# A transformer layer with 32 experts: small loads moved behind the first projection's input, the last output tiles taken half by half up to the gather, and the overflow path's loads on another queue

## The chip, the cores and the metric

The kernel runs on one core of a Trainium2 chip. The core has five engines with a queue of instructions each: TensorE (PE, with its weight loads as PEld), VectorE (DVE), ScalarE (ACT), GpSimd (POOL) and SyncE (SP). Loads from memory are issued from an engine's queue; here SP issues the large ones and ACT the small ones. The metric is the device time of one execution in microseconds (us).

## The reference

One decoder layer over 256 tokens of width 1024:

```python
mod = silu(c) @ w_ada + b_ada            # shifts, scales and gates
h = x * (1 + scale) + shift              # adaLN
proj = h @ w_in                          # attention, indexer and retention heads
mix = concat(sparse_attention(proj), retention(proj))
x = layer_norm(x * ALPHA + gate * (mix @ w_out))
# top-4 of 32 experts, clamped SwiGLU, 1024 -> 2 x 1024 -> 1024
x = layer_norm(x * ALPHA + gate2 * moe(x))
```

The sparse attention keeps the 64 best keys of a token by an indexer's score and adds a bias by distance. Each expert has 12 MB of weights in float32 (`w_gate_up` 8 MB, `w_down` 4 MB), and all 32 are read once.

## The kernel before

**Front.** TensorE forms the shifts and scales `sha` and `sc1` from eight tiles of `w_ada` of 1 MB (`mod_step`, L163). ACT and DVE then make `h` from `xT` in two parts: `hh` (ACT, L238) is `h` rounded, `hl` (DVE, L240) what rounding lost, over the full value `hfull` (L239). Weights are split the same way into `whi` and `wlo` (`split`, L258 and L259), and `proj_t` adds `whi`·`hh`, `whi`·`hl` and `wlo`·`hh`. The first two tiles so used are `w_idx` (result in `ps_g`, then `wiT`, L313) and the first `w_in` tile (result in `pq`, then `qiT`, L319). The profile gives matmuls the line of their helper `mm`, L110.

**Loads.** `load` issues on SP's queue, `small` on ACT's. Small tensors are loaded at the start: `head`, `hot`, `row`; then `fd` (written to memory, L193) and `bias` (read back from it in another layout, L196), the constants `cst` (L211), `b_ada` (L215) and `rows_` (L217). SP and ACT take eight completion semaphores (DMAHW0 to DMAHW7 in the listings) in turn; a load takes one only when the load that had it before has landed.

**Output and routing.** Four tiles of `w_out` cover pairs of `k`: `out_all(i)` does pair `i` for both halves of the tokens (`s`) and of the width (`j`), with three products for each `k` into `pz[s][j]`. For the last pair a loop over `s` and `j` does `out_proj((6, 7), s, j)`, then `z` (L600, L601), its statistics (L607), its transposes `pn` (L604), `zT`, and the router's logits; for each `s` it then makes the choice of the experts (`msk`, L624), the rank of a token at its expert (`prk` on TensorE, `rk`, L630) and the normalized rows `nh` and `nl` (L633). `dispatch(0)` compares ranks with slots (`oh`, L736) and gathers the first four experts' tokens by matmul (`pg`), copied out as `xe` (L749, L751).

**Experts.** A ring of 17 slots of 1 MB holds weight tiles; `load_up` (L706) and `load_down` (L714) issue a tile when a slot is free. TensorE does `pgate`, `pup` and `py`. After expert 24 a flag `over` is read, and `tc.If` (L960) runs `overflow()` if some expert got more tokens than it has slots for. Ahead of the `If`, the loads of expert 25 and of `w_down` of 24 are issued as `ahead`.

Of the kernel before, what the change touches and what calls it, by code (L numbers as in the profile page):

```python
# [14 lines left out]
OP = mybir.AluOpType  # L15
# [78 lines left out]
def layer(ctx, tc, t, out):  # L94
# [116 lines left out]
    small(out=cst, in_=t["cst"])  # L211
# [91 lines left out]
    with tc.issue_after(first["mod"].ins):  # L303
# [3 lines left out]
    w = w_in("p (k c) -> p k c", k=8)  # L307
    idx = scr6[:, 0:1024].rearrange("p (i c) -> p i c", i=4)
# [263 lines left out]
    out_all(2)  # L572
# [20 lines left out]
    for s in range(2):  # L593
        st = sb("lst", 128, 2, 6, bufs=2)
        pr = ps("s")
        z = acc[:, s]
        for j in range(2):
            js = slice(j * 512, (j + 1) * 512)
            out_proj((6, 7), s, j)
            V.tensor_mul(z[:, js], pz[s][j], ga[:, js])  # L600
            V.scalar_tensor_tensor(z[:, js], xn[s][:, js], ALPHA, z[:, js], op0=OP.mult, op1=OP.add)  # L601
            pn = ps("t", (128, 4, 128), name="pn")
            for b in range(4):
                T.transpose(pn[:, b], z[:, j * 512 + b * 128:j * 512 + (b + 1) * 128], ident)  # L604
            zT = sb("zT", 128, 4, 128, bufs=2)
            A.activation(zT, pn, AF.Copy)
            V.bn_stats(st[:, j], z[:, js])  # L607
            for b in range(4):
                k = 4 * j + b
                mm(pr[:, 0:E], zT[:, b], w_ha[:, k], k == 0, k == 7)  # L610
        mv = sb("lmv", 128, 2, bufs=2)
        V.bn_aggr(mv, st)
        sd = sb("lsd", 128, 2, bufs=2)
# [16 lines left out]
        V.scalar_tensor_tensor(rk[:, s], prk[:, 0:E], 1.0, msk[:, s], op0=OP.add, op1=OP.mult)  # L630
        nl.append(sb(f"nl{s}", 128, D, pool=keep, dt=F32R, tag=f"x{s}"))
        with tc.issue_after(placed.ins):
            V.scalar_tensor_tensor(nl[s], z, sd[:, 0:1], nh[:, s].bitcast(F32), op0=OP.mult, op1=OP.subtract)  # L633
            V.tensor_copy(rstd[:, s:s + 1], sd[:, 0:1])
# [95 lines left out]

    def dispatch(quad):

        e = 4 * quad
        oh = mk.tile([128, 2, 4, CAP], F32R, name="oh", bufs=1)
        for s in range(2):
            V.tensor_tensor(oh[:, s], slots[:, None, :].to_broadcast([128, 4, CAP]),  # L736
                            rk[:, s, e:e + 4, None].to_broadcast([128, 4, CAP]), op=OP.is_equal)
        xes = [mk.tile([128, 8, 128], F32, name="xe", bufs=3) for _ in range(2)]
        pgs = []

        def gather(i, s, start, stop):
# [4 lines left out]
        def take(h, i, engine):
            src = pgs[i // 2][:, i % 2, 128 * h:128 * h + 128]
            if engine is V:
                return V.tensor_scalar(xes[h][:, i], src, ha[:, i:i + 1], hb[:, i:i + 1], op0=OP.mult, op1=OP.add)  # L749
            else:  # L750
                return A.activation(xes[h][:, i], src, AF.Identity, bias=hb[:, i:i + 1], scale=ha[:, i:i + 1])  # L751

        if quad == 0:

            for s in range(2):
                for i in range(8):
                    if s == 0 and i % 2 == 0:
                        pgs.append(ps("t" if i < 4 else "g", (128, 2, 256), name="pg"))
                    gather(i, s, s == 0 and i % 2 == 0, s == 1 and i % 2 == 1)
            for h in range(2):  # L760
                for i in range(8):
                    first[i % 2] = take(h, i, (V, A)[i % 2])
        else:
            for i in range(8):
                if i % 2 == 0:
                    pgs.append(ps("t", (128, 2, 256), name="pg"))
                for s in range(2):
                    gather(i, s, s == 0, s == 1)
            for i in range(8):
                for h in range(2):  # L770
                    take(h, i, (V, A)[h])
# [325 lines left out]
```

## Time and profile before

| what | value |
|---|---|
| runs | 1153.84, 1156.03, 1156.25 us (median 1156.03) |
| the profiled execution | 1154.32 us, span 1152.6 us |
| PE busy | 1048.8 us (91%) |
| DVE, ACT, POOL busy | 358.6, 177.5, 50.9 us |
| moved | 451.99 MB, 392 GB/s on average |

The span runs from the first to the last instruction. The share of busy time is an average over stages with different limits; each stage has to be read by itself, by which wait ends last in it.

### The profile page before, as it was taken

Reading aid. Unit: us, or ns where it says so; the run is one execution under the profiler, and the core shown is the slowest. Engines: PE = TensorE matmul, PEld = TensorE weight load, DVE = VectorE, ACT = ScalarE, POOL = GpSimd, SP = SyncE. Lnnn points to the kernel's source line nnn. Section 1 sums busy time; section 2 is a strip of 40 time slices with the busy share of each in tenths; the row PEclk is TensorE's granted clock in tenths of the full one; section 3 lists DMA queues with packets and bytes.
Section 4 is the critical chain, followed back from the end, with each engine's and each line's share of the span. In section 5 each row is a group of like instructions: output and inputs, shape, how many; then the busy total and the mean of one; then the engine's idle time right before and its main releaser. Section 6 shows DMA issues by size and latency. Waiting matters only on the chain. (4 is left out here: it accounts for less than half of the span.)

```text
span 1152.6 us, 12061 instructions
## 1 busy us (share of the span) xinstructions
PE 1048.8 (91%) x4939; PEld 449.1 (39%) x4939; DVE 358.6 (31%) x665; ACT 177.5 (15%) x292; POOL 50.9 (4%) x38
## 2 busy tenths in 40 slices
PE   7799997999999999999999899989988698999895
PEld 1587686443434333432333233323422133443232
DVE  0586785312222222321222122212221211312125
ACT  1424641400201000100010001000100000200001
POOL 0114210110000000000000000000000000000001
PEclk9799997999999999999999999999999989999998
DMA  9968995799999999999999999999999989999994
GB/s 357 374 238 345 338 397 220 298 412 421 421 421 421 422 421 421 421 422 421 421 422 421 421 422 421 421 422 421 421 421 422 421 331 423 421 421 421 421 418 162
DMA packets 65861, 451.99 MB, mean 392 GB/s; under 512 B 7380, under 2 KB 8573, under 8 KB 11817
## 3 DMA queue, kind: packets, MB, share of 16 engines
q1 hardware_dynamic: 63536, 447.52, 94.3%
q10 hardware_dynamic: 2266, 3.65, 1.0%
q8 instruction: 41, 0.67, 0.2%
q14 instruction: 18, 0.15, 0.0%
HBM read 450.05 MB, written 1.09 MB: 391 GB/s over the span
## 5 line engine op out<-in xcount | busy, mean ns | idle before, releaser
L110 PE MATMUL pgate<-w,xe 128*64 128x512 f32 x1024 | 345.3, 604 | 27.7 <-DMA w<-in_w_gate_up 27.7
L110 PE MATMUL pup<-w,xe 128*64 128x512 f32 x1024 | 352.2, 596 | 0.0
L110 PE MATMUL py<-w,aT 128*64 128x512 f32 (+1 forms) x1056 | 244.0, 592 | 11.1 <-DMA w<-in_w_down 9.4
L110 PEld LDWEIGHTS pgate<-w,xe 128*64 128x64 f32 x1024 | 93.6, 137 | 177.0 <-DMA w<-in_w_gate_up 83.2
L110 PEld LDWEIGHTS pup<-w,xe 128*64 128x64 f32 x1024 | 104.7, 137 | 145.9 <-issue 139.4
L800 DVE TENSOR_SCALAR sw_g<-pgate 128x512 f32<-128x512 f32 x32 | 22.1, 692 | 384.8 <-PE pgate L110 384.8
L110 PEld LDWEIGHTS py<-w,aT 128*64 128x64 f32 x1056 | 71.6, 137 | 140.0 <-issue 93.0
L846 DVE TENSOR_TENSOR y<-py,gf 64x512 f32<-64x512 f32 x62 | 42.7, 688 | 206.5 <-PE py L110 206.1
L801 ACT ACTIVATE act<-sw_g 128x512 f32<-128x512 f32 x32 | 20.2, 630 | 511.4 <-DVE sw_g L800 511.4
L873 DVE TENSOR_TENSOR acc<-acc,psc 128x512 f32<-128x512 f32 x60 | 38.6, 684 | 24.5 <-PE psc L110 24.5
L749 DVE TENSOR_SCALAR xe<-pg,ha,hb 128x128 f32<-128x128 f32 x64 | 25.6, 409 | 57.2 <-PE pg L110 43.8
L1026 POOL TENSOR_TENSOR acc<-acc,ln 128x512 f32<-128x512 f32 (+1 forms) x2 | 2.7, 1340 | 908.1 <-ACT acc L1025 908.1
L110 PE MATMUL pm<-w,cT 128*32 128x512 f32 x192 | 35.8, 726 | 5.8 <-DMA w<-in_w_ada 5.8
L751 ACT ACTIVATE xe<-pg,hb,ha 128x128 f32<-128x128 f32 x64 | 28.4, 458 | 63.8 <-DVE xe L749 63.8
L258 ACT ACTIVATE whi<-w 128x2048 fp32r<-128x2048 f32 (+1 forms) x17 | 31.3, 1839 | 40.2 <-DMA w<-lay_w_in 11.4
L110 PE MATMUL pg<-oh,nh 128*128 128x256 f32 x128 | 35.6, 310 | 1.1 <-DVE oh L736 1.1
L860 ACT ACTIVATE yh<-y,gs 128x1024 fp32r<-128x1024 f32 x15 | 17.2, 1148 | 110.9 <-DVE y L846 110.9
L110 PE MATMUL pg<-oh,nl 128*128 128x256 f32 x128 | 34.2, 298 | 0.0
L829 ACT ACTIVATE aT<-pact 128x512 f32<-128x512 f32 x32 | 19.1, 597 | 98.0 <-PE pact L828 98.0
L110 PE MATMUL psc<-yh,ohT 128*128 128x512 f32 x60 | 24.9, 455 | 10.1 <-ACT yh L860 6.8
L259 DVE TENSOR_TENSOR wlo<-w,whi 128x2048 fp32r<-128x2048 f32 (+1 forms) x14 | 30.9, 2209 | 4.4 <-ACT whi L258 4.2
L110 PEld LDWEIGHTS <-pick 96*64 96x64 bf16 x190 | 15.0, 109 | 44.1 <-issue 40.5
(260 smaller groups left out, 911.0 us busy)
## 6 DMA issues: line engine op xcount, KB each, us to landing
w<-in_w_gate_up SPq DMA_DIRECT2D x256, 1024.0 KB, 19.8
w<-in_w_down SPq DMA_DIRECT2D x124, 1024.0 KB, 19.8
w<-in_w_ada SPq DMA_DIRECT2D x24, 1024.0 KB, 7.0
w<-lay_w_in SPq DMA_DIRECT2D x12, 1024.0 KB, 9.2
w<-lay_w_out SPq DMA_DIRECT2D x4, 1024.0 KB
w<-in_w_down SPq DMA_DIRECT2D x7, 512.0 KB, 17.0
bias<-fd ACTq DMA_DIRECT2D x1, 1024.0 KB, 14.2
xT<-lay_xT SPq DMA_DIRECT2D x1, 1024.0 KB, 8.7
```

What stands on the lines that cost most here:

```text
L110: T.matmul(o, l, r, start=start, stop=stop)
L258: A.activation(hi, w, AF.Copy)
L259: (G if i % 4 == 3 and i < 13 else V).tensor_tensor(lo, w, hi.bitcast(F32), op=OP.subtract)
L749: return V.tensor_scalar(xes[h][:, i], src, ha[:, i:i + 1], hb[:, i:i + 1], op0=OP.mult, op1=OP.add)
L751: return A.activation(xes[h][:, i], src, AF.Identity, bias=hb[:, i:i + 1], scale=ha[:, i:i + 1])
L800: V.tensor_scalar(g, pg, 7.0, None, op0=OP.min)
L801: A.activation(s, g, AF.Sigmoid, scale=1.702)
L829: A.activation(aT, pa, AF.Copy)
L846: V.tensor_mul(y[o:o + CAP, c], py[64 * c:64 * c + 64], gf[64 * c:64 * c + 64, c * 512:(c + 1) * 512])
L860: A.activation(yh, y, AF.Copy, scale=gs)
L873: V.tensor_add(o, o, p_)
L1026: G.tensor_mul(o, o, g2[:, cs])
```

## The change

Five parts. `load_later()` issues `cst`, `fd`, `b_ada`, `rows_` and `bias` behind the copy of `whi` of the first `w_in` tile on ACT. `hh` is made first, half on ACT and half on DVE, and then `hfull` and `hl` in pairs; `proj_t` does all eight products with `hh` before those with `hl`. `out_all(2)` is gone: with TensorE's order written out by hand, `out_proj` takes pairs 2 and 3 (`k` = 4 to 7) for one (`s`, `j`) at a time, and transposes, logits, ranks and both parts of the first gather follow in that order. The overflow path's loads go on POOL's queue. `ahead` is gone.

```diff
+    def load_later():
+        fap = fd[:]
+        small(out=cst, in_=t["cst"])
+        small(out=fd, in_=f8)
+        small(out=b_ada[0:128:32], in_=t["b_ada"])
+        small(out=bias, in_=bass.AP(tensor=fap.tensor, offset=fap.offset, ap=[[1, 128], [384, H], [1, 256]]))
+        small(out=rows_[0:72], in_=t["rows"])
...
     for b in range(8):
         if b % 2 == 0:
-            f2 = sb("hfull", 128, 2, 256, bufs=2, tag="zT")
-        f = f2[:, b % 2]
-        A.activation(hh[:, b], xT[:, b], AF.Identity, bias=sha[:, b:b + 1], scale=sc1[:, b:b + 1])
-        V.tensor_scalar(f, xT[:, b], sc1[:, b:b + 1], sha[:, b:b + 1], op0=OP.mult, op1=OP.add)
-        V.tensor_sub(hl[:, b], f, hh[:, b].bitcast(F32))
+            A.activation(hh[:, b], xT[:, b], AF.Identity, bias=sha[:, b:b + 1], scale=sc1[:, b:b + 1])
+        else:
+            first["h"] = V.tensor_scalar(hh[:, b], xT[:, b], sc1[:, b:b + 1], sha[:, b:b + 1], op0=OP.mult, op1=OP.add)
+    for b in range(0, 8, 2):
+        f2 = sb("hfull", 128, 2, 256, bufs=2, tag="zT")
+        V.tensor_scalar(f2[:, 0], xT[:, b], sc1[:, b:b + 1], sha[:, b:b + 1], op0=OP.mult, op1=OP.add)
+        A.activation(f2[:, 1], xT[:, b + 1], AF.Identity, bias=sha[:, b + 1:b + 2], scale=sc1[:, b + 1:b + 2])
+        V.tensor_sub(hl[:, b:b + 2], f2, hh[:, b:b + 2].bitcast(F32))
...
     w = w_in("p (k c) -> p k c", k=8)
+    with tc.issue_after(first["split"].ins):
+        load_later()
...
     split_wo(3)
-    out_all(2)
...
+    with tc.manual_schedule(engines={mybir.EngineType.PE}):
+        for j in range(2):
+            out_proj((4, 5, 6, 7), 0, j)
+            z_out(0, j)
+        zT0 = z_T(0, 0)
+        out_proj((4, 5), 1, 0)
+        logits(0, 0, zT0)
+        zT1 = z_T(0, 1)
+        out_proj((6, 7), 1, 0)
+        z_out(1, 0)
+        logits(0, 1, zT1)
+        stats(0)
+        out_proj((4, 5), 1, 1)
+        zT0 = z_T(1, 0)
+        out_proj((6, 7), 1, 1)
+        first["z"] = z_out(1, 1)
+        choose(0)
+        logits(1, 0, zT0)
+        rank(0)
+        zT1 = z_T(1, 1)
+        stats(1)
...
+        logits(1, 1, zT1)
+        choose(1)
...
-                        nc.sync.dma_start(out=w, in_=t["w_gate_up"][0, bass.ds(e, 1), k * 128:(k + 1) * 128,
+                        G.dma_start(out=w, in_=t["w_gate_up"][0, bass.ds(e, 1), k * 128:(k + 1) * 128,
...
-        if e == E - 7:
-            wu, wd = ahead
-        else:
-            wu = load_up(e)
-            wd = load_down(e - 1) if e else None
+        wu = load_up(e)
+        wd = load_down(e - 1) if e else None
...
         if e == E - 8:
-            ahead = load_up(e + 1), load_down(e)
             r = nc.values_load(over[0:1, 0:1], min_val=0, max_val=1)
```

On ACT near the start, the rows of before, from the store of `fd` to the load of `rows_` (`pd` is a small matmul's result, DMA a load's issue, the numbers behind names are of buffers):

```order
L193 DMA fd_97<-scr7_69 8x384 [waits DVE_49]
L211 DMA cst_117<-lay_cst 128x1072
L203 ACTIVATE scr8_70<-pd_101 128x256 [waits PE_49]
L196 DMA bias_99<-fd_97 128x8x256 [waits DMAHW5_49]
L203 ACTIVATE scr8_70<-pd_104 128x256 [waits PE_49]
L203 ACTIVATE scr8_70<-pd_107 128x256 [waits PE_49]
L215 DMA b_ada_92<-lay_b_ada 4x1024 [waits DMAHW2_49,Pool_49]
L203 ACTIVATE scr8_70<-pd_110 128x256 [waits PE_49]
L209 ACTIVATE scr9_71<-ps_t_114 128x512 [waits DMAHW3_49,PE_49]
L217 DMA rows__120<-lay_rows 72x512 [waits DMAHW4_49]
```

The five loads stand between the first copies out of TensorE, ahead of the copy of `modrow` that leads to `sha`. In the changed kernel, from the last copies of `hfull`:

```order
L263 ACTIVATE whi_239<-w_237 128x2048 [waits DMAHW5_49]
L244 ACTIVATE hfull_198<-xT_117,sha_176,sc1_177 128x256 [waits DVE_49]
L244 ACTIVATE hfull_202<-xT_117,sha_176,sc1_177 128x256 [waits DVE_49]
L197 DMA cst_115<-lay_cst 128x1072 [waits DMAHW0_49]
L198 DMA fd_97<-scr7_69 8x384
L199 DMA b_ada_92<-lay_b_ada 4x1024 [waits Pool_49]
L201 DMA rows__116<-lay_rows 72x512 [waits DMAHW6_49]
L200 DMA bias_98<-fd_97 128x8x256 [waits DMAHW7_49,DMAHW2_49]
L321 ACTIVATE scr6_72<-ps_g_212 4x256 [waits DVE_49,PE_49]
L327 ACTIVATE scr6_72<-pq_251 128x256 [waits PE_49]
L327 ACTIVATE scr6_72<-pq_251 128x256
L263 ACTIVATE whi_389<-w_387 128x2048
```

They now stand behind `hh`, `hfull` and `whi`, ahead of the copies for `wiT` (L321) and `qiT` (L327), with a wait for `fd` ahead of the load of `bias`; the copy of the next `whi` stands behind the copies of `qiT`.

On TensorE at the end of the output projection, the rows of before from the first transposes of `s`=1 to the gather (`ps_s` the logits, `pn` the transposes, `prk` the rank); the last product `pz` and the rank of `s`=0 stand right ahead of them:

```order
L604 MATMUL pn_1528<-head_73,acc_1288 128x128 [waits PE_49]
L604 MATMUL pn_1528<-head_73,acc_1288 128x128 x3
L604 MATMUL pn_1548<-head_73,acc_1288 128x128 [waits DVE_49]
L604 MATMUL pn_1548<-head_73,acc_1288 128x128
L110 MATMUL ps_s_1519<-w_ha_1330,zT_1533 128x32 [waits Activation_49]
L110 MATMUL ps_s_1519<-w_ha_1330,zT_1533 128x32 x3
L604 MATMUL pn_1548<-head_73,acc_1288 128x128 x2
L110 MATMUL prk_1574<-msk_1453,ones_82 128x32 [waits PE_49]
L110 MATMUL ps_s_1519<-w_ha_1330,zT_1553 128x32 [waits Activation_49]
L110 MATMUL ps_s_1519<-w_ha_1330,zT_1553 128x32 x3
L110 MATMUL prk_1574<-msk_1453,cst_117 128x32 [waits DVE_49]
L110 MATMUL pg_1596<-oh_1591,nh_1289 128x256 [waits DVE_49,PE_49]
```

All of `s`=1's transposes, logits and rank stand behind the last product, and the gather behind both ranks.

Changed, from the last four products to the start of the gather (`pr` now names the logits):

```order
L110 MATMUL pz_1331<-wlo_1407,ch_1176 128x512
L110 MATMUL pz_1331<-whi_1406,ch_1176 128x512
L110 MATMUL pz_1331<-whi_1406,cl_1209 128x512
L110 MATMUL pz_1331<-wlo_1407,ch_1176 128x512
L110 MATMUL pr_1429<-w_ha_1326,zT_1522 128x32 [waits Activation_49]
L110 MATMUL pr_1429<-w_ha_1326,zT_1522 128x32 x3
L110 MATMUL prk_1543<-msk_1425,cst_115 128x32 [waits DVE_49,PE_49]
L615 MATMUL pn_1546<-head_73,acc_1284 128x128 [waits DVE_49,PE_49]
L615 MATMUL pn_1546<-head_73,acc_1284 128x128 x3
L110 MATMUL pr_1429<-w_ha_1326,zT_1551 128x32 [waits Activation_49]
L110 MATMUL pr_1429<-w_ha_1326,zT_1551 128x32 x3
L110 MATMUL pg_1573<-oh_1434,nh_1285 128x256 [waits DVE_49]
```

The transposes of `s`=1's first half stand six products ahead of the logits, the rank of `s`=0 stands right behind the first four logits of `s`=1, and the gather of `s`=0 (`nh`, `nl0`) ahead of the rank of `s`=1.

On SP at the `If`, before, from the last load ahead of it to the false path's jump:

```order
L714 DMA w_4862<-in_w_down 128x2048 [waits DMAHW1_49,PE_49]
L714 DMA w_4864<-in_w_down 128x2048 [waits DMAHW2_49,PE_49]
L959 TENSOR_LOAD over_1585 [waits DVE_49]
L960 COMPARE_AND_BRANCH
...
L960 UNCONDITIONAL_BRANCH [waits DMAHW0_49,DMAHW1_49,DMAHW2_49,DMAHW3_49,DMAHW4_49,DMAHW5_49,DMAHW6_49,DMAHW7_49]
```

The jump past the overflow path waits for all eight completion semaphores, behind twelve loads. Changed:

```order
L783 DMA w_4739<-in_w_down 128x2048 [waits DMAHW6_49,PE_49]
L1009 TENSOR_LOAD over_1623 [waits DVE_49]
L1009 ISA x2
L775 DMA w_5204<-in_w_gate_up 128x2048 [waits DMAHW7_49,PE_49]
L775 DMA w_5206<-in_w_gate_up 128x2048 [waits DMAHW0_49,PE_49]
L775 DMA w_5208<-in_w_gate_up 128x2048 [waits DMAHW1_49,PE_49]
L775 DMA w_5210<-in_w_gate_up 128x2048 [waits DMAHW2_49,PE_49]
L1010 COMPARE_AND_BRANCH
...
L1010 UNCONDITIONAL_BRANCH
L775 DMA w_5212<-in_w_gate_up 128x2048 [waits DMAHW3_49,PE_49]
```

Four loads of the next expert stand between the read of the flag and the branch, the jump waits for nothing, and the other loads stand behind it.

## Rows read from the trace of the kernel before

**Rows 1.** The page, part 4: chain that ended last, by line

```profile
DMA w<-in_w_gate_up 10%; DMA w<-in_w_down 3%; PE py L110 1%; PE pgate L110 1%; PE pup L110 1%; PE p L110 0%; PE pg L110 0%; DVE acc L1021 0%; PE psc L110 0%; DVE acc L1020 0%; DVE y L996 0%; DVE yl L998 0%; ACT yh L997 0%; PE pact L828 0%; DVE fst L1016 0%; SPq L706 0%
```

**Rows 2.** Windows: length, busy us (and count) per engine, TensorE clock, DMA share, GB/s

```profile
0.00:20.00 20.00, 12.89 (x34) 3.72 (x38) 1.26 (x5) 3.02 (x6) 2.86 (x13) 1.00 0.91 365
20.00:30.00 10.00, 7.39 (x38) 1.43 (x38) 0.00 (x0) 0.60 (x1) 0.00 (x0) 1.00 0.88 313
60.00:180.00 120.00, 119.54 (x760) 89.90 (x758) 88.03 (x175) 49.80 (x77) 29.52 (x16) 1.00 0.86 330
200.00:210.00 10.00, 10.00 (x55) 6.24 (x55) 4.42 (x20) 6.43 (x13) 0.00 (x0) 0.84 0.19 66
930.00:940.00 10.00, 10.00 (x48) 3.51 (x47) 0.00 (x0) 0.00 (x0) 0.00 (x0) 0.99 0.69 287
940.00:950.00 10.00, 10.00 (x51) 3.49 (x49) 2.67 (x4) 1.23 (x2) 0.00 (x0) 1.00 0.74 305
960.00:1110.00 150.00, 141.32 (x608) 53.06 (x608) 35.80 (x57) 16.75 (x28) 0.00 (x0) 0.98 1.01 421
```

**Rows 3.** Timeline of SP's DMA queue: start, length, line, count

```profile
17.89 10.82 SPq L163 DMA_DIRECT2D w<-in_w_ada  x2
```

**Rows 4.** Waits of SP, 0 to 40 us: total, times, longest us

```profile
SPq L163 <- DMA bias<-fd: 10.1, 1, 10.1
SPq L163 <- DMA fd<-scr: 5.9, 1, 5.9
```

**Rows 5.** Timeline of ACT and its DMA queue, 0 to 60 us

```profile
9.17 0.29 ACTq L193 DMA_DIRECT2D fd<-scr  x1
...
14.20 0.44 ACTq L196 DMA_DIRECT2D bias<-fd  x1
...
50.70 1.91 ACT L258 ACTIVATE whi<-w 128x2048 fp32r<-128x2048 f32 x1 [3.93 <-PE pq L110]
```

**Rows 6.** Timeline of PE, 26 to 60 us; in brackets the idle time before, and releaser

```profile
25.81 1.58 PE L110 MATMUL pm<-w,cT 128*32 128x512 f32 x11
...
33.23 1.93 PE L110 MATMUL pm<-w,cT 128*32 128x512 f32 x8 [5.84 <-DMA w<-in_w_ada]
...
53.07 1.73 PE L110 MATMUL psc<-scr 64*128 64x128 f32 x16 [1.29 <-ACT scr L319]
```

**Rows 7.** Timeline of DVE, 30 to 60 us

```profile
37.01 0.16 DVE L230 TENSOR_TENSOR sha<-pmt,head 128x8 f32<-128x8 f32 x1
...
42.31 0.75 DVE L240 TENSOR_TENSOR hl<-hfull,hh 128x256 fp32r<-128x256 f32 x2
```

**Rows 8.** Timeline of PE, 170 to 212 us

```profile
185.14 0.40 PE L110 MATMUL pz<-wlo,ch 128*128 128x512 f32 x1
...
188.39 0.38 PE L110 MATMUL prk<-msk,cst 128*128 128x32 f32 x2 [2.85 <-DVE msk L624]
...
198.18 0.55 PE L110 MATMUL pg<-oh,nh 128*128 128x256 f32 x1 [1.13 <-DVE oh L736]
...
204.84 1.03 PE L110 MATMUL pgate<-w,xe 128*64 128x512 f32 x4
```

**Rows 9.** Timeline of DVE, 170 to 212 us

```profile
172.47 2.29 DVE L259 TENSOR_TENSOR wlo<-w,whi 128x2048 fp32r<-128x2048 f32 x1 [0.82 <-ACT whi L258]
...
196.26 1.28 DVE L633 SCALAR_TENSOR_TENSOR nl<-acc,lsd,nh 128x1024 fp32r<-128x1024 f32 x1
...
197.62 0.75 DVE L736 TENSOR_TENSOR oh<-slots,rk 128x256 fp32r<-128x256 f32 x2
```

**Rows 10.** Waits of SP, 900 to 945 us

```profile
SPq L960 <- SPq L960: 19.5, 3, 14.5
```

**Rows 11.** Timeline of SP's DMA queue, 890 to 960 us

```profile
912.54 7.78 SPq L714 DMA_DIRECT2D w<-in_w_down  x4
...
941.22 4.04 SPq L706 DMA_DIRECT2D w<-in_w_gate_up  x8
```

**Rows 12.** Timeline of PE, 900 to 960 us

```profile
924.65 0.64 PE L110 MATMUL pgate<-bias_gu,pick 96*64 96x512 bf16 x2 [5.27 <-PEq L960]
```

More of the change, by code (lines that the diff above doesn't have):

```diff
@@ L302, in layer @@
     load(out=w, in_=t["w_idx"])
-    with tc.issue_after(first["mod"].ins):
+    with tc.issue_after(first["mod"].ins), tc.issue_after(first["h"].ins):
         w = [d.rearrange("p (k c) -> p k c", k=8) for d in split(w)]
@@ L592, in layer @@
     rstd = sb("rstd", 128, 2, pool=keep)
[L593 to L613, printed above, removed]
+    prs = [ps("s", name="pr") for _ in range(2)]
@@ L630, in layer, with low, one_hot, gather @@
         V.scalar_tensor_tensor(rk[:, s], prk[:, 0:E], 1.0, msk[:, s], op0=OP.add, op1=OP.mult)
+    def low(s):
         nl.append(sb(f"nl{s}", 128, D, pool=keep, dt=F32R, tag=f"x{s}"))
-        with tc.issue_after(placed.ins):
-            V.scalar_tensor_tensor(nl[s], z, sd[:, 0:1], nh[:, s].bitcast(F32), op0=OP.mult, op1=OP.subtract)
-            V.tensor_copy(rstd[:, s:s + 1], sd[:, 0:1])
+        V.scalar_tensor_tensor(nl[s], acc[:, s], sds[s][:, 0:1], nh[:, s].bitcast(F32), op0=OP.mult, op1=OP.subtract)
+    def one_hot(quad, s):
+        V.tensor_tensor(oh[:, s], slots[:, None, :].to_broadcast([128, 4, CAP]),
+                        rk[:, s, 4 * quad:4 * quad + 4, None].to_broadcast([128, 4, CAP]), op=OP.is_equal)
+    def gather(i, s, start, stop):
+        for n in (nh[:, s], nl[s]):
+            mm(pgs[i // 2][:, i % 2], n[:, i * 128:(i + 1) * 128], oh[:, s].rearrange("p e c -> p (e c)"),
+               start and n is not nl[s], stop and n is nl[s])
+    oh = sb("oh", 128, 2, 4, CAP, pool=keep, dt=F32R)
+    with tc.manual_schedule(engines={mybir.EngineType.PE}):
[19 more added lines that the diff above has]
+        stats(1)
+        with tc.issue_after(first["z"].ins):
+            low(0)
+            one_hot(0, 0)
+        logits(1, 1, zT1)
+        choose(1)
+        for i in range(8):
+            if i % 2 == 0:
+                pgs.append(ps("g" if i < 4 else "t", (128, 2, 256), name="pg"))
+            gather(i, 0, i % 2 == 0, False)
+        rank(1)
+        with tc.issue_after(first["chosen"].ins):
+            low(1)
+            one_hot(0, 1)
+        for i in range(8):
+            gather(i, 1, False, i % 2 == 1)
+    for s in range(2):
+        V.tensor_copy(rstd[:, s:s + 1], sds[s][:, 0:1])
     gate = sb("gate", 128, 2, E, pool=keep)
@@ L729, in down_rows, with take, new_xes @@
         return t["w_down"][0, e, i * 256:(i + 1) * 256, :].rearrange("(p j) c -> p j c", j=2)
+    def take(xes, h, i, engine):
+        src = pgs[i // 2][:, i % 2, 128 * h:128 * h + 128]
+        if engine is V:
+            return V.tensor_scalar(xes[h][:, i], src, ha[:, i:i + 1], hb[:, i:i + 1], op0=OP.mult, op1=OP.add)
+        return A.activation(xes[h][:, i], src, AF.Identity, bias=hb[:, i:i + 1], scale=ha[:, i:i + 1])
+    def new_xes():
+        return [mk.tile([128, 8, 128], F32, name="xe", bufs=3) for _ in range(2)]
@@ L746, in take @@
[L746 to L749, printed above, removed]
-            else:
-                return A.activation(xes[h][:, i], src, AF.Identity, bias=hb[:, i:i + 1], scale=ha[:, i:i + 1])
-        if quad == 0:
+            one_hot(quad, s)
+        xes = new_xes()
+        pgs.clear()
+        for i in range(8):
+            if i % 2 == 0:
+                pgs.append(ps("t", (128, 2, 256), name="pg"))
@@ L755, in dispatch @@
             for s in range(2):
[L756 to L759, printed above, removed]
+                gather(i, s, s == 0, s == 1)
+        for i in range(8):
             for h in range(2):
[L761 to L771, printed above, removed]
@@ L922, in overflow @@
                     V.scalar_tensor_tensor(o, tm, gc[:, s:s + 1], o, op0=OP.mult, op1=OP.add)
-    xes, oh = dispatch(0)
+    xes = new_xes()
+    for h in range(2):
+        for i in range(8):
+            first[i % 2] = take(xes, h, i, (V, A)[i % 2])
     acts = {}
```

77 lines of the change are left out of this document (44 added, 33 removed).

## Prediction

> **What bounds the kernel now.** I read the chain that ended last first: it is weight transfers of the experts, `w_gate_up` before `w_down` [rows 1]. Then windows, with the share of DMA time: from 960 to 1110 us the DMA engines are busy 1.01 at 421 GB/s, while TensorE is busy 141.3 of 150 us waiting for tiles [rows 2]. So in the expert stage a microsecond is gained only where DMA stands still, and every microsecond by which the ring of weight tiles starts to turn earlier is a microsecond of the end. The same table shows where DMA stands still: 20 to 30 us (0.88), 200 to 210 us (0.19), and 930 to 950 us (0.69 and 0.74, so 5.7 us lost). Between 60 and 180 us DMA is not the limit (0.86) but TensorE is: 119.5 of 120 us busy. Hence three places, in series: the front (until TensorE runs without a break), the routing (until expert 0 frees ring slots), the branch after expert 24. What is won in each adds up, if the cover between them holds.
>
> The profiled execution took 1154.3 us, 1.7 us over its span of 1152.6; the median of the three runs is 1156.0, 1.7 above the profiled one. I make the sum against 1154.3 and add 1.7.
>
> **Part 1, late small loads behind `h`.** The eighth `w_ada` tile is issued only at the end of the SP row that starts at 17.89 and lasts 10.82 us [rows 3]. The reason stands in SP's waits: 10.1 us for `bias`<-`fd` and 5.9 us for `fd` [rows 4], since SP and ACT take the same eight completion semaphores in turn, and a load takes one again only when its last user has landed. `fd` was issued at 9.17 and `bias`, which reads it, at 14.20 [rows 5], so `fd` took 5.0 us. TensorE then waits 5.84 us for that tile and resumes at 33.23 [rows 6]; `sha` follows at 37.01 [rows 7]. After the change the first loads wait for small loads that landed long before. What must land for `sha` is 8 `w_ada` tiles, `xT` and 0.13 MB of small tensors, 9.57 MB; in the first 20 us DMA moves 7.30 MB (365 GB/s [rows 2]); the remaining 2.27 MB at 0.42 MB/us end at 25.4, with 0.5 to 1.5 us of tail at 26 to 27, against 33.23. From there to `sha` before: 3.8 us, of which the eight products of the tile took 1.93, where eleven took 1.58 before the wait [rows 6]; at that pace it would be 3.0. So `sha` comes at 29 to 30.8 against 37.0: gain 6.2 to 8, I take 7.3.
>
> **Part 2, `h` in another order.** DVE now has, after `sha`, 4 `hh`, 4 `hfull`, 4 `hl` of double width and both `wlo`. Two `hl` took 0.75 us [rows 7]; at 0.35 each for the 256 columns of `hh` and `hfull`, twice that for a double `hl` and for the narrow `wlo` (estimates from that row), and 2.29 for the wide `wlo` (as in [rows 9]), the last `hl` is done at `sha` + 8.6; before, it was at 43.1, `sha` + 5.9. TensorE can do all products with `hh` in between, and has 34 matmuls left after the last `hl`. Before, `sha` to the end of these products and the small transposes behind them took 14.6 us (53.07 less 1.29 [rows 6]) for 72 matmuls, 0.2 each. 34 at 0.13, were there no more waits and a full clock, end at `sha` + 13.1, at 0.2 at + 15.4. I take 13.9: 0.7 us gained (bounds -0.8 and +1.5). On ACT the split copy of 1.91 us that stood ahead of the `qiT` copies (50.70 [rows 5]) now stands behind them; this ends the 1.29 us that TensorE waited there [rows 6], but its `wlo` (2.29) then comes later: net gain 0.2 to 1. DVE's scores begin about 2 us later against TensorE; before, TensorE waited for nothing from 60 to 180 us, so the slack there is unknown: 0 to 2 us lost. I take 1. Front: 7.3 + 0.7 + 0.5 - 1 = 7.5, bounds 3.5 (6.2 - 0.8 + 0.2 - 2) and 9.5 (all high ends, less 1).
>
> The moved loads (1.8 MB) now run on ACT's queue beside SP's `w_in` tiles. I cost them at nothing, because from 60 us on DMA runs below its limit (0.86) and TensorE never waits [rows 2]; `bias` waits for `fd` on ACT's in-order queue, and behind it stand the `wiT` and `qiT` copies. `fd` issued near `sha` + 6 and 5.0 us long lands at + 11, the copies of `qiT` are wanted near + 13.9: 3 us of cover. If it is gone, each us is lost.
>
> **Part 3, `w_out` half by half, gather early.** Before, the last `pz` ends at 185.54 (E), and expert 0 starts at 204.84 [rows 8]: 19.3 us, in which lie the choice and rank of `s`=0, all of `s`=1's logits, choice and rank, and then the 32 gathers. Waits stand in it: 2.85 us for `msk` and 1.13 for `oh` [rows 8] among them. Now TensorE takes tiles 4 to 7 of one (`s`,`j`) together. Cost: the last `wlo` (172.47 + 2.29 = 174.76 [rows 9]) was covered by the 24 products of `out_all(2)`; now it is wanted after 8, so TensorE stalls about 10 products, 2.4 us, of which the moved `pw` (0.8) fill a third: 1.6 us. One more group of transposes lies ahead of E: 0.4. E becomes 187.4 in the old time. Behind it there is left, from durations of rows 8 and 9: DVE finishes `z` (1.5), then `rk`, statistics, `nl0` (1.28), `oh` (0.75 for two) and the subtraction, 3.1 together; the choice of `s`=1 (1.3); `nl1`, `rk`, `oh` (196.26 to 198.0, 1.7). That is E + 7.6. Transposes, logits and the 16 gathers of `s`=0 lie beside it on TensorE. Then 16 gathers: before, 32 took from 198.18 to 204.4 [rows 8], 0.19 each with a granted clock of 0.84 over the window from 200 [rows 2], so partly at the lower of its two levels, 1.2 GHz, and partly at 2.4. 16 take 3.1 in that mixture; an estimate for more of the one or the other level is 1.9 to 3.4. With 0.4 to the first expert product: E + 9.9 to 11.4, up to 13.5 if the lower clock lets the first gathers delay the rank. So 197.3 to 200.9 against 204.84: gain 3.9 to 7.5; I take 6, bounds 3 and 7.5. All of it passes: DMA is empty then (0.19), with all 17 slots filled, and restarts when expert 0 frees the first.
>
> **Part 4, overflow loads on POOL's queue.** Before, the false path of the `If` makes SP wait for all eight completion semaphores: 19.5 us [rows 10]; SP issues four loads at 912.54 to 920.3 and none until 941.22 [rows 11]. DMA runs dry for 5.7 us of that [rows 2]. Now SP's branch has no such wait, and POOL's has nothing in flight. TensorE still waits 5.27 us at its own branch [rows 12]; with tiles landing meanwhile that is covered by the ring (17 tiles of 2.49 us, 42 us). I take 5.7, bounds 4 and 6.5.
>
> **Sum.** 7.5 + 6 + 5.7 = 19.2; 1154.3 - 19.2 + 1.7 = 1136.8, about 1137. The low ends (3.5 + 3 + 4 = 10.5) give 1145.5, the high ends (23.5) 1132.5.
>
> **The rivals.** Below 0.2% (2.3 us) a measurement of this kernel doesn't tell a change from none.
>
> *A. Forecast, all three pass*: 1133 to 1142, chance 0.62.
>
> *B. The late loads take the front's gain back.* 1.8 MB beside `w_in` at 0.42 MB/us are 4.3 us, if TensorE waits for `w_in` there, and `fd` may hold ACT. For it: in the front DMA has little to spare (0.91 and 0.88 with its gaps [rows 2]). Against it: TensorE did not wait at all from 60 us on. The front then gives 2 to 3: 1142. Chance 0.13. The Trainium skill, "DMA: Bandwidth & Descriptors", section "Queues, rings and completion order", says that each DMA engine goes round between the queue rows that have work, packet by packet, so ACT's small loads would not wait behind SP's tiles but take turns with them; the rows of before agree in so far as `fd`, issued beside full SP traffic, landed in 5.0 us; by it B's price, 4.3 us, would fall on the `w_in` tiles.
>
> *C. The branch still drains DMA.* SP, too, must fetch and jump; if it pauses as TensorE did (5.27) and what is in flight is short, 3 to 6 us stay: 1142 to 1144. For it: TensorE's row; against it: SP has eight loads in flight, some 20 us. Chance 0.08. The Trainium skill, "Runtime: NRT & Kernel Launch", section "Instruction fetch mechanics", says that a taken branch out of the fetched window makes the engine fetch by DMA before it goes on; SP would be no exception.
>
> *D. Routing gains nothing.* The `wlo` stall and half clock eat it: TensorE at E + 15 or later: 1142 to 1144. Chance 0.09.
>
> *E. Slower.* Completion semaphores again: SP's `w_in` loads now wait for `cst`, `fd`, `b_ada` and `bias`, which land only after `h`. If `bias` lands so late that SP stands and the `w_in` tiles miss TensorE by over 19 us + 2.3, that is more than 21 us (`bias` at about 75 instead of some 54), the kernel is slower: 1160 with five more. Against it: `fd` took 5.0 us, and `bias` by SP's waits some 14. Chance 0.04. Remaining 0.04: several of B, C, D together, 1146 to 1153, or no change.
>
> **How the numbers follow.** The likeliest is A: 1137. Two in ten outside: 1130 (all high ends and 2.5 us more, as a starved DMA may give more than its windows show) to 1146 (the low ends, or B with part of C or D). Faster 0.93, within 0.2% 0.03, slower 0.04.
>
> **What would show it.** Right: no SP wait for `bias` before 30 us, TensorE's wait before the last `pm` under 2 us, `sha` near 30; first expert product 12 us earlier than before; no SP wait at the `If` and DMA at 1.0 in the windows of the branch. Wrong: TensorE idle on `w_in` between 45 and 70 us (B), a gap in DMA after expert 24 (C), TensorE waiting for `wlo` or DVE over 4 us in the routing (D), SP waiting for `bias` past 60 us (E).

## The result, and the profile after

The changed kernel takes 1136.25 us (median of four runs, 1135.27 to 1137.54) against 1156.14 us for the kernel before in the same comparison: ratio 0.9833, 95% interval 0.9816 to 0.985. A second comparison gave 1137.48 us and a ratio of 0.9853 (0.9837 to 0.987). The forecast was 1137. The profiled execution took 1137.54 us, the slowest of the four, with a span of 1135.9, so the two spans differ by 16.7 us and the medians by 19.9.

**Front.** The timeline of DVE shows `sha` (ahead of it, in [rows 7], 37.01):

```profile
29.88 0.16 DVE L232 TENSOR_TENSOR sha<-pmt,head 128x8 f32<-128x8 f32 x1
```

SP's DMA queue: the last `w_ada` tiles for it, and the `w_in` tile issued latest in this stretch; then SP's wait for it:

```profile
7.40 0.86 SPq L163 DMA_DIRECT2D w<-in_w_ada  x2
...
42.31 0.33 SPq L271 DMA_DIRECT2D w<-lay_w_in  x1
```

```profile
SPq L271 <- DMA cst<-lay_cst: 12.3, 1, 12.3
```

The eighth tile is issued at 8.3 us, where [rows 3] had it at 28.7. PE's timeline shows what follows:

```profile
23.62 4.77 PE L110 MATMUL pm<-w,cT 128*32 128x512 f32 x34
...
45.09 1.68 PE L110 MATMUL psc<-scr 64*128 64x128 f32 x16
```

All products of `w_ada` now run without a wait to 28.4, and `psc` starts at 45.09 against 53.07 [rows 6]: 8.0 us earlier, of which `sha` has 7.1. The other 0.9 us is not the new order of `h`: with the late loads alone `psc` starts at 44.82. The new waits lie on SP and ACT. SP stands 12.3 us for `cst`, whose completion semaphore the next `w_in` tile takes; the tile is issued at 42.31. ACT's timeline shows the other:

```profile
34.00 0.35 ACTq L197 DMA_DIRECT2D cst<-lay_cst  x1
34.39 0.34 ACTq L198 DMA_DIRECT2D fd<-scr  x1
...
41.68 0.41 ACTq L200 DMA_DIRECT2D bias<-fd  x1
42.19 0.38 ACT L321 ACTIVATE scr<-ps_g 4x256 f32<-4x256 f32 x1 [6.28 <-DMA rows__116<-lay_rows]
44.00 0.66 ACT L327 ACTIVATE scr<-pq 128x256 f32<-128x256 f32 x2 [1.44 <-PE pq L110]
```

`fd` took 7.3 us (34.39 to 41.68, 5.0 before [rows 5]). A reason stands in the order of ACT's queue: `cst` (536 KB) is now issued ahead of `fd`, where before it came behind it, and the trace's packets have most of `cst` from 37.51 to 40.03 us and the first of `fd` at 39.87. ACT stood 6.28 us in front of the copy for `wiT`, because `bias` waits for `fd` ahead of it. The copies of `qiT` were still on time: ACT waited 1.44 us for their products. So the cover that I gave as 3 us was 1.4.

**Routing.** PE's timeline from the stall for the last `wlo` to expert 0:

```profile
167.55 0.50 PE L110 MATMUL pz<-wlo,ch 128*128 128x512 f32 x1 [1.07 <-DVE wlo L264]
...
179.74 0.40 PE L110 MATMUL pz<-wlo,ch 128*128 128x512 f32 x1
...
182.15 0.63 PE L615 MATMUL pn<-head,acc 128*128 128x128 f32 x4 [0.97 <-DVE acc L609]
...
185.25 0.41 PE L110 MATMUL pg<-oh,nh 128*128 128x256 f32 x1
185.46 0.41 PE L110 MATMUL pg<-oh,nl 128*128 128x256 f32 x1
...
189.30 0.36 PE L110 MATMUL pg<-oh,nh 128*128 128x256 f32 x1 [0.28 <-DVE oh L656]
...
191.36 1.08 PE L110 MATMUL pgate<-w,xe 128*64 128x512 f32 x4
```

Before, from the last `wlo` (174.76 [rows 9]) to the end of the last product it took 10.8 us, and from there to expert 0's first product 19.3 [rows 8]. Now it takes 12.7 (`wlo` is done at 167.49) and 11.2: the stall and one more group of transposes cost 1.9, the rest gives 8.1. At 191.36 the kernel is 13.5 us ahead of before. The gathers at 185.25 are 0.21 us apart at a granted clock of 0.5, those of `s`=1 0.12 apart.

**Windows**, of the same columns as [rows 2]:

```profile
20.00:30.00 10.00, 9.15 (x58) 2.38 (x50) 0.63 (x3) 0.93 (x2) 0.00 (x0) 1.00 1.02 418
40.00:50.00 10.00, 9.98 (x79) 8.50 (x78) 4.34 (x6) 6.16 (x9) 1.63 (x3) 1.00 0.74 268
60.00:165.00 105.00, 104.18 (x662) 76.61 (x661) 79.79 (x153) 46.19 (x73) 28.02 (x16) 1.00 0.91 348
...
210.00:220.00 10.00, 10.00 (x33) 3.47 (x34) 1.38 (x2) 1.19 (x2) 5.04 (x3) 0.90 0.69 269
...
900.00:910.00 10.00, 4.52 (x8) 2.17 (x8) 4.54 (x6) 1.15 (x1) 0.00 (x0) 0.57 1.01 420
910.00:920.00 10.00, 7.78 (x32) 2.94 (x34) 0.00 (x0) 0.00 (x0) 0.00 (x0) 0.74 1.01 418
920.00:930.00 10.00, 10.00 (x52) 4.14 (x49) 0.98 (x2) 1.02 (x2) 0.00 (x0) 1.00 1.01 420
```

DMA has no gap at 20 to 30 us (1.02, before 0.88) and none at the branch (1.01, 1.01, 1.01; before 0.69 and 0.74). Between expert 0 and 1 the gap at 210 to 220 us is wider: 269 GB/s against the 421 of a full window make 3.6 us; before, 369 and 371 GB/s in the windows 220 to 230 and 230 to 240 made 2.4 in the same place of the program. The granted clock of this window is 0.90; in the second profile of the changed kernel, at 1.00, the gap is 1.9 us, so the change does not widen it every time. SP's own branch lies in the first of the following rows of its DMA queue, with four loads ahead of it and four behind; the row is as long as the last one, which has no branch. TensorE waits at its branch as in [rows 12]:

```profile
879.83 17.77 SPq L775 DMA_DIRECT2D w<-in_w_gate_up  x8
899.72 7.83 SPq L783 DMA_DIRECT2D w<-in_w_down  x4
909.71 18.85 SPq L775 DMA_DIRECT2D w<-in_w_gate_up  x8
...
940.85 17.74 SPq L775 DMA_DIRECT2D w<-in_w_gate_up  x8
```

```profile
912.22 0.64 PE L110 MATMUL pgate<-bias_gu,pick 96*64 96x512 bf16 x2 [5.36 <-PEq L1010]
```

Landmarks with the same work behind them: at the first issue of `w_down` of expert 24 the kernel is 12.8 us ahead (899.72 against 912.54 [rows 11]), at the end 16.7. So DMA's idle time at the branch is gone, 5.9 us by its bytes, but the end gained only 3.9 there. The difference is there at once: at the first `w_gate_up` load of expert 27 the kernel is 16.5 us ahead (940.85 against the row of before below), and at the first `w_down` load of expert 30 it is still 16.5 (1080.14 against 1096.66).

```profile
957.35 2.82 SPq L706 DMA_DIRECT2D w<-in_w_gate_up  x2
```

### The profile page after: what moved, and what is told of

Read it like the earlier page. It is cut to its first block, busy times and chain, and to the rows that moved or that the text cites. A ratio compares the mean times of both kernels' runs of the same rounds, so it can differ in the third digit from the quotient of the medians.

```text
span 1135.9 us, 12046 instructions
## 1 busy us (share of the span) xinstructions
PE 1044.3 (92%) x4939; PEld 440.9 (39%) x4939; DVE 360.4 (32%) x661; ACT 177.4 (16%) x292; POOL 49.4 (4%) x38
## 4 chain that ended last, share of the span: by engine, by line
DMA 57%; PE 36%; DVE 4%; ACT 1%; issue 1%; SPq 0%; ACTq 0%; DVEq 0%
DMA w<-in_w_gate_up 37%; DMA w<-in_w_down 19%; PE py L110 7%; PE pgate L110 7%; PE pup L110 6%; PE pm L110 3%; PE pr L110 2%; PE pv L110 2%; PE pz L110 2%; PE pg L110 1%; PE psc L110 1%; PE pb L110 1%; PE pq L110 1%; PE pact L879 1%; DVE wlo L264 1%
## 5 line engine op out<-in xcount | busy, mean ns | idle before, releaser
L110 PE MATMUL pgate<-w,xe 128*64 128x512 f32 x1024 | 341.4, 604 | 24.5 <-DMA w<-in_w_gate_up 24.4
L110 PE MATMUL pup<-w,xe 128*64 128x512 f32 x1024 | 347.4, 594 | 0.0
L110 PEld LDWEIGHTS pup<-w,xe 128*64 128x64 f32 x1024 | 101.2, 137 | 148.5 <-issue 144.7
L110 PEld LDWEIGHTS pgate<-w,xe 128*64 128x64 f32 x1024 | 90.5, 136 | 173.4 <-issue 92.5
## 6 DMA issues: line engine op xcount, KB each, us to landing
w<-in_w_down SPq DMA_DIRECT2D x7, 512.0 KB, 12.7
```

What stands on the lines that cost most here:

```text
L110: T.matmul(o, l, r, start=start, stop=stop)
```

## The experiments

Ratios are of the kernel before on the same chip. The first four do one part each.

**Late loads alone.** Only `load_later()` and its place.

```diff
+    with tc.issue_after(first["split"].ins):
+        load_later()
```

> Before, with only the small loads moved behind h. Theory (parts add up): the eighth w_ada tile is no longer held by bias, sha comes about 7 us earlier (near 30 instead of 37.0) and this passes to the end: 7 us faster, about 1149 us. Rival (the moved loads take it back): fd holds ACT in front of the copies for wiT and qiT, or cst and bias hold SP's w_in loads, and TensorE waits: 2 to 3 us faster, about 1153.5 us, with an idle time of TensorE over 3 us between sha and the first psc that before did not have.

Measured: 0.9933 (0.9919 to 0.9947), 1147.09 us, 7.7 us faster. `sha` comes at 29.67. The theory holds, the rival doesn't.

**Order of `h` alone.**

```diff
             mm(po, hi[:, k, c0:c0 + m], hh[:, k], k == 0, False)
+        for k in range(8):
             mm(po, hi[:, k, c0:c0 + m], hl[:, k], False, False)
...
```

To this come the loops that make `hh` first.

> Before, with only the order of hh, hfull, hl and of the products in proj_t changed. Theory: sha stays at 37, from sha to the next pq after psc it takes about 0.9 us less: 0.5 to 1 us faster, 1155.3 us, hardly to be told from no change. Rival (the order is what makes the front short): 3 us or more faster, 1153 us or less.

Measured: 1.0003 (0.9993 to 1.0013), no difference. TensorE's wait for the `qiT` copies is shorter (0.31, before 1.29 [rows 6]), but `psc` starts no earlier:

```profile
51.79 1.05 PE L110 MATMUL pm<-w,cT 128*32 128x512 f32 x2
53.15 1.73 PE L110 MATMUL psc<-scr 64*128 64x128 f32 x16 [0.31 <-ACT scr L323]
```

The shorter wait is no gain by itself, since two products of `w_ada` (1.05 us) now stand in it. `sha` came at 37.54 in this execution; from `sha` to `psc` it takes 15.61 us, before 16.06, which is half of the 0.9 us that the theory had, and too little for the times to show.

**Routing alone**: the hand-written order from the output projection to the gather, the rest as before.

```diff
-    out_all(2)
+    with tc.manual_schedule(engines={mybir.EngineType.PE}):
+        for j in range(2):
+            out_proj((4, 5, 6, 7), 0, j)
+            z_out(0, j)
...
```

> Before, with only the output tiles half by half and the gather placed early. Theory: from the last wlo to expert 0's first product it takes about 6.2 us less, and all of it passes, because DMA stands still with 17 full slots: 1150 us. Rival (given back behind the routing, where DMA has a second gap between expert 0 and 1): 3 to 4 us faster, 1152.5 us.

Measured: 0.9955 (0.9938 to 0.9972), 1150.06 us, 5.2 us faster. The interval reaches from 3.2 to 7.2, so it holds the theory's 6.2 and does not shut the rival's 3 to 4 out; from the last product to expert 0 it is 11.2 us as in the full change. The profiled execution took 1154.41 us, the slowest of six (1147.73 to 1154.41), and its span of 1152.7 shows no gain at the end. It was 4.8 us late already when the last `wlo` was done (179.54, before 174.76), with a wait of TensorE of 3.0 us for DVE that before does not have and whose cause is open. From there to expert 0 it takes 23.9 us, before 30.1: the 6.2 of the theory.

**Branch alone.**

```diff
-            nc.sync.dma_start(out=bgd[0:4], ...
+            G.dma_start(out=bgd[0:4], ...
...
-            ahead = load_up(e + 1), load_down(e)
```

> Before, with only the overflow loads on POOL's queue and no loads ahead of the If. Theory (DMA engines drift apart when they are not drained): DMA's idle time of 5.7 to 5.9 us at the branch is gone, but the end comes only 3.6 to 4.2 us earlier, about 1152.2 us, and DMA's busy share falls step by step over the last 10 us of the weight loads instead of at once. Rival (the idle time is all there is): 5.7 us faster, 1150.4 us, with a sharp end of the loads.

Measured: 0.9964 (0.9951 to 0.9976), 1150.81 us, 4.2 us faster (2.8 to 5.7); the spans differ by 3.7 (1148.9 against 1152.6). DMA is at 1.01 or more in all windows from 900 to 950. The interval reaches the rival's 5.7, so the time does not decide, but the rows of the end do. Windows of 6 us, from 30 to 18 us before the end of the span, first of before, then of the branch alone, then of the full change; the last two columns are DMA's share and GB/s:

```profile
1122.60:1128.60 6.00, 6.00 (x34) 2.02 (x30) 1.38 (x2) 0.00 (x0) 0.00 (x0) 1.00 1.04 386
1128.60:1134.60 6.00, 4.80 (x38) 2.36 (x34) 1.60 (x3) 0.72 (x1) 0.00 (x0) 1.00 0.80 293
```

```profile
1118.90:1124.90 6.00, 6.00 (x32) 1.98 (x30) 1.38 (x2) 0.00 (x0) 0.00 (x0) 1.00 1.03 379
1124.90:1130.90 6.00, 4.80 (x40) 2.40 (x36) 1.60 (x3) 0.72 (x1) 0.00 (x0) 1.00 0.48 181
```

```profile
1105.90:1111.90 6.00, 6.00 (x32) 1.97 (x30) 1.38 (x2) 0.00 (x0) 0.00 (x0) 1.00 1.03 381
1111.90:1117.90 6.00, 4.80 (x40) 2.40 (x36) 1.60 (x3) 0.72 (x1) 0.00 (x0) 1.00 0.56 208
```

TensorE does the same there (6.00 and 4.80 us busy), so these windows lie at the same place of the program. In before DMA works at 0.80 of the second window, in the two others at 0.48 and 0.56: some of the 16 engines are done earlier, while the last tile lands at the same distance from the end. That is 0.24 to 0.32 of 6 us, 1.4 to 1.9 us in which DMA is not full.

The trace also holds what none of these views lists: a load of 1 MB leaves sixteen updates of its completion semaphore, as many as there are DMA engines. In before, from the first to the last of a load's updates it takes 5.7 us ahead of the branch (median of the loads that landed between 870 and 915 us) and 2.0 near the end (1060 to 1100); with the branch alone it takes 5.8 and 7.5. At the drain of before, the first updates of two loads in turn are 11.6 us apart and the last ones 5.7, where otherwise both are 2.5: the earliest engines stood 9.1 us, the latest 3.2. TensorE takes a tile only when its last part has landed (the last update of one came at 900.06 us, its first product at 900.11), so a standstill of 5.9 us on average held the kernel up by less.

The next four take the full change and undo or move something.

**Old branch put back**, the last diff turned round.

> The changed kernel with the old branch put back (overflow loads on SP's queue, two groups of loads ahead of the If). Theory (drift): DMA stands still some 5.9 us behind expert 24, but the end is only 3.6 to 4.2 us later, about 1140.2 us, and the weight loads end sharply. Rival (idle time is all): 5.9 us later, 1142 us.

Measured: 0.9881 (0.9866 to 0.9896), 1142.1 us. That is the rival's time and not the theory's 1140.2; against the full change's two ratios it is 3.2 or 5.5 us slower, each uncertain by some 2.6 us (an estimate from the intervals), which shuts neither out. Its windows behind expert 24, and at the end:

```profile
920.00:930.00 10.00, 10.00 (x50) 3.66 (x46) 1.16 (x2) 0.60 (x1) 0.00 (x0) 1.00 0.44 184
930.00:940.00 10.00, 10.00 (x51) 4.04 (x51) 2.89 (x5) 0.63 (x2) 0.00 (x0) 1.00 0.98 382
```

```profile
1110.70:1116.70 6.00, 6.00 (x34) 2.02 (x32) 1.38 (x2) 0.00 (x0) 0.00 (x0) 1.00 1.04 386
1116.70:1122.70 6.00, 4.80 (x38) 2.37 (x34) 1.60 (x3) 0.72 (x1) 0.00 (x0) 1.00 0.81 296
```

DMA loses 6.6 us there (5.6 + 0.9 by GB/s) and the span is 4.8 or 6.0 us longer than in the two profiles of the full change. The end of the loads is full again (0.81), as the theory had it.

**Old branch, behind expert 8.**

```diff
-        if e == E - 8:
+        if e == 8:
+            ahead = load_up(e + 1), load_down(e)
...
```

> The changed kernel with the old branch put back, but behind expert 8 instead of 24. Theory (DMA engines drift apart again after a drain, little by little): what the drain gives back is lost again by the end; DMA stands still for some 5.9 us and the end is 5 us or more later than the changed kernel, 1141.5 to 1142.5 us, with a stepwise end of the loads. Rival (what is given back lies with TensorE or the tail and has nothing to do with the drain's place): the same as with the old branch behind expert 24, about 1140.

Measured: 0.9882 (0.9867 to 0.9897), 1141.67 us, 3.3 or 5.7 us slower than the full change: the time forecast by the theory, but also that of the old branch behind expert 24, so the times don't tell the two apart. The rows do:

```profile
440.00:450.00 10.00, 10.00 (x44) 3.55 (x42) 0.00 (x0) 0.00 (x0) 0.00 (x0) 0.84 0.63 229
```

```profile
1109.90:1115.90 6.00, 6.00 (x33) 2.03 (x30) 1.38 (x2) 0.00 (x0) 0.00 (x0) 1.00 1.04 385
1115.90:1121.90 6.00, 4.80 (x38) 2.34 (x32) 1.60 (x3) 0.72 (x1) 0.00 (x0) 1.00 0.56 206
```

The gap behind expert 8 costs 4.6 us, less than the 6.6 behind expert 24, and the loads end unevenly (0.56). From the first to the last of a load's sixteen updates it takes 1.7 us behind this drain (460 to 520 us) and 5.1 again near the end. So the even end hangs on a drain late in the program; all profiles with the old branch behind expert 24 show 0.79 to 0.81, all without it 0.48 to 0.56.

**Small loads back at the start**, the first diff turned round.

> The changed kernel with the small loads back at the start. Theory (parts add up): the eighth w_ada tile waits for bias again, sha comes 7 us later and so does the end: 1143 us. Rival (the small loads only moved the contention, the order of h is what counts): 2 to 3 us later, 1139 us.

Measured: 0.9925 (0.9911 to 0.9939), 1145.77 us: 8.3 or 10.6 us slower than the full change, more than the theory's 7 and far from the rival's 2 to 3. SP waits 10.4 us for `bias` again. The parts stand in series: alone, the four give 7.7, -0.3, 5.2 and 4.2, together 16.8; the full change gave 17.0 and 19.3.

**The gap between expert 0 and 1.** TensorE frees no slot for some 10 us there, with broadcasts for the residual and for `gf`.

```diff
...
-                residual()
...
             down(e - 1, a, y, wd)
+            if e == 1:
+                residual()
```

One of its tiles also takes another buffer.

> The changed kernel with the first layer norm's residual (four broadcasts by TensorE, eight matmul records of about 0.5 us) moved from between expert 0 and 1 to behind expert 0's down projection. Theory: DMA's second gap behind the routing (2.9 us, at 214 to 219 us) comes from TensorE freeing no slot for 10 us; 4 us less of other work there closes the gap: 2 to 3 us faster than the changed kernel, about 1133.5 us. Rival (the drift of the DMA engines or TensorE's later wait takes it): less than 0.7 us, 1136.

Measured: 0.9839 (0.9826 to 0.9852), 1137.51 us: no gain, as the rival had it, though the gap was gone. The same kernel again, beside the full change on one chip:

> The kernel with the residual moved behind expert 0's down projection again. In its first profile DMA's gap between expert 0 and 1 was gone (3.6 us), but expert 0 began 13.9 us behind the last output product instead of 11.6, at a granted clock of 0.5. Theory (that clock was that execution's): 2 to 3 us below the changed kernel of this call. Rival (moving the residual brings the lower clock, or the end does not follow the gap): within 0.7 us of it.

The full change unaltered:

> The changed kernel again, beside the next three on one chip. Both theories: ratio 0.981 to 0.985 to before, some 1136 us; expert 0's first product 11.2 us behind the last output product, as in the first profile.

Measured: 0.9854 (0.984 to 0.9867) with the residual moved and 0.9853 (0.9837 to 0.987) for the full change, which lies at the slow end of what was expected of it: no gain again. The two expectations count from the start of the last product; from its end it now takes 13.3 us to expert 0, against 10.3 in the full change beside it, which ran at a granted clock of 1.0 there, and 11.2 in its first profile, which did not. A part of the cause stands in DVE's timeline, first of this kernel, then of the full change's first profile:

```profile
188.10 0.19 DVE L649 SCALAR_TENSOR_TENSOR rk<-prk,msk 128x32 f32<-128x32 f32 x1 [2.01 <-PE prk L110]
188.21 1.27 DVE L653 SCALAR_TENSOR_TENSOR nl<-acc,lsd,nh 128x1024 fp32r<-128x1024 f32 x1
189.40 0.42 DVE L656 TENSOR_TENSOR oh<-slots,rk 128x256 fp32r<-128x256 f32 x1
```

```profile
186.34 1.28 DVE L653 SCALAR_TENSOR_TENSOR nl<-acc,lsd,nh 128x1024 fp32r<-128x1024 f32 x1
188.50 0.19 DVE L649 SCALAR_TENSOR_TENSOR rk<-prk,msk 128x32 f32<-128x32 f32 x1 [0.88 <-PE prk L110]
188.73 0.42 DVE L656 TENSOR_TENSOR oh<-slots,rk 128x256 fp32r<-128x256 f32 x1
```

DVE's order has changed: `nl` of 1.27 us stands behind `rk`, between it and `oh`, where the full change does it during the wait for the rank. In both, `rk` comes 8.4 us behind the last product, but `oh` comes 1.1 us later here and expert 0 2.1 us. TensorE was also at the lower clock for longer in both profiles of the moved residual; here ten of the sixteen gathers of `s`=1 run some 0.2 us apart instead of 0.12, about the rest of the 2.1. The edit closed one gap and opened another of about its size.

**Broadcasts of `gf` in TensorE's waits.**

```diff
...
         rank(0)
+        gf_row(0)
         zT1 = z_T(1, 1)
+        gf_row(1)
...
-                for j in range(2):
-                    bcast_row(gf[:, j * 512:(j + 1) * 512], rowc, 2 + j, 1.0)
```

> The changed kernel with the two broadcasts of gf (2 us of TensorE) moved from behind expert 0 into TensorE's waits of the routing (0.97 and 0.75 us, behind the rank of s=0 and behind the last transposes). Theory (the waits are free, and DMA's gap between expert 0 and 1 shrinks by what is moved): 1 to 2 us below the changed kernel of this call. Rival (the copies on ACT and the broadcasts delay the chain to the rank): expert 0 starts 1 us later, no gain or 0.5 us slower.

Measured: 0.9822 (0.9808 to 0.9835), 1133.91 us, 3.6 us below the full change beside it, whose interval (0.9837 to 0.987) it just doesn't touch; with that of the full change's first comparison (0.9833, 0.9816 to 0.985) it overlaps. PE's timeline:

```profile
180.53 1.10 PE L110 MATMUL pb<-modrow,head 128*128 128x512 f32 x2
181.67 0.63 PE L615 MATMUL pn<-head,acc 128*128 128x128 f32 x4
182.13 1.02 PE L110 MATMUL pb<-modrow,head 128*128 128x512 f32 x2
...
184.16 0.28 PE L110 MATMUL pg<-oh,nl 128*128 128x256 f32 x1
184.28 0.28 PE L110 MATMUL pg<-oh,nh 128*128 128x256 f32 x1
...
189.91 1.08 PE L110 MATMUL pgate<-w,xe 128*64 128x512 f32 x4
```

The broadcasts fill the waits, `pg` runs 0.12 us apart, and the granted clock is 1.0 throughout; the gap behind expert 0 falls to 0.8 us. Expert 0 starts 10.3 us behind the last product, as in the full change profiled beside it (which kept its clock too), so of the 3.6 the profile shows about 1.1 from the gap, and the two spans differ by 1.7. Another part goes with the clock: of the four executions of the full change beside it, those with a mean granted clock of 0.985 and 0.984 took 1136.38 and 1136.08 us, those with 0.983 and 0.979 took 1138.58 and 1139.58. That the broadcasts keep the clock up is not shown, since the full change kept it without them in its second profile.

**Both moves**, the last two diffs together.

> Both moves, residual and gf. Theory: DMA has no gap between expert 0 and 1; 3 us below the changed kernel of this call, 1133 us. Rival: the lower clock in the routing or the soft end takes it: within 1 us of the changed kernel.

Measured: 0.9827 (0.9804 to 0.9851), 1134.07 us, span 1132.7. No gap is left between expert 0 and 1, and it is 3.0 us below the full change by the ratios, as the theory had it, but the broadcasts alone give as much. DVE's order is again that of the full change and expert 0 starts 10.6 us behind the last product, so moving the residual does not by itself cost the 3 us seen above. The broadcasts alone are the version to take.

## Why the prediction was right

- **Part 1, 7.3 us for `sha`:** 7.1 in the profile; the loads alone gave 7.7. The chain (semaphore, eighth tile, `sha`) was as told. The cover for `bias` was 1.4 us and not 3, in part since `fd` stood behind `cst`. Rival B didn't come: `cst` held a `w_in` tile for 12.3 us, but TensorE was busy 9.98 of 10 us at 40 to 50 us. By the rule of the Trainium skill, "DMA: Bandwidth & Descriptors", section "Queues, rings and completion order", ACT's small loads take turns with SP's tiles. The trace agrees only in part: `fd`, issued 4.7 us behind an SP tile (34.39 and 29.66), landed 0.3 us ahead of it (41.66 and 41.93), but its 12 KB took 7.3 us, more than the 5.0 that I had used.
- **Part 2, 0.2 us net** (0.7 + 0.5 - 1): nothing measurable alone; the profile has 0.45 from `sha` to `psc`. The last `hl` was done 8.6 us behind `sha` as forecast (37.17 + 1.29 = 38.46 against 29.88). The low bound of the front adds up to 3.6 and not 3.5 (6.2 - 0.8 + 0.2 - 2). The loss of 1 us by later scores was not measured apart.
- **Part 3, 6 us:** E came 1.9 later than before relative to the last `wlo` (2.0 forecast), expert 0 at E + 11.2 (9.9 to 11.4 forecast; 10.3 in the second profile, at a granted clock of 1.0), 6.2 us net; alone it measured 5.2. Rival D didn't come: TensorE stood 1.07 us for the last `wlo`. Not foreseen: DMA's gap between expert 0 and 1, where TensorE's broadcasts free no slot, took 3.6 us instead of 2.4 in the first profile (1.9 in the second). I wrote that all of it passes, because I looked at DMA up to the first freed slot only.
- **Part 4, 5.7 us:** the idle time is gone as forecast (5.9), but the term was too large: the end gained 3.9 in the profile, 4.2 measured alone. "A microsecond is gained where DMA stands still" fails here by 1.4 to 1.9 us, because the standstill also let all DMA engines start again together: the sixteen parts of a load came 5.7 us apart ahead of it and 2.0 near the end, and the latest engine stood 3.2 us of the mean 5.9. The mean share of DMA, from which the 5.7 was taken, hides that. The time of the old branch put back, 1142.1 us, fits the full 5.9 as well. Rival C didn't come: SP shows no wait at its branch, TensorE 5.36 us. The Trainium skill, "Runtime: NRT & Kernel Launch", section "Instruction fetch mechanics", says that a taken branch out of the fetched window costs a fetch; the trace agrees for TensorE, in whose 5.36 us a packet of 16 KB on the instruction queue starts (909.6 us), and for SP no run here shows it.
- **Rival E** didn't come: no row shows SP waiting for `bias`.

The sum of the profile is 7.3 (at the last `wlo`) + 6.2 - 0.7 (lost from expert 0 to 24) + 3.9 = 16.7, against 19.2 forecast. The median lay 19.9 below, since the profiled execution of before was at the fast end of its runs and that of after at the slow end of its own. The parts measured alone make 16.8 and the second comparison 17.0. So the mechanisms held, but that the forecast time came within 1 us of the measured one is luck: the overestimate for the branch lies within what single executions differ by.

## What to carry to other kernels

Look at which semaphore, buffer or queue an early large load shares with a small slow one: here a load that nobody needed yet held 7 us of the front. Where a stage waits for a chain on other engines, put into the waits what would come right behind: here it did not delay the chain, and it shrank a gap that had opened later. After moving work, read the order on every engine again: a scheduler may put a moved step's neighbours into the chain.

## What was not expected of the hardware

A drain of all loads late in the program makes the last loads end together: DMA's share in the same window is 0.79 to 0.81 with it and 0.48 to 0.56 without, in five profiles of the former kind and nine of the latter. From the first to the last of a load's sixteen updates it takes 1.8 to 2.0 us near the end in the five, 5.1 to 7.9 in the nine. It grows in steps: from 240 to 1100 us the fourteen traces have 56 steps of more than 0.5 us from one load to the next, and all of them come 2.1 to 4.2 us behind the start of a packet of 16 KB on the queue that the page calls `q8 instruction`, although only some 17% of the loads land within 5 us of one. There are 41 such packets in before, of about 1 us each. So the loading of instructions is the likely cause; that such a packet holds up one engine alone is not shown, as the trace doesn't name its engine. Removing a standstill of 5.9 us gave 3.7 to 4.2. The granted clock in the routing differed between two executions of one kernel (0.5, the lower of its two levels, for some 3.5 us, or 1.0 throughout), with the same instructions in the same order. With TensorE's waits filled it stayed at 1.0 in both profiles, but two profiles without that kept it too, so no cause is shown.
